# A third FFN pair computed by quarters, and a gate held until after m5's copy, in a one-core encoder block

## The chip, the cores and the metric

The kernel runs on one core of a Trainium2 chip. The metric is the time of one execution on the device, in microseconds. The core's engines are TensorE (PE in the profile, its weight loads PEld), VectorE (DVE), ScalarE (ACT), GpSimd (POOL) and SyncE (SP, which here only issues loads). Each engine runs its own instructions in order and waits on semaphores for the others.

## The reference

One layer over 512 tokens of width 1024, in float32. Two of its stages are gated FFNs with a hidden width of 2816, and the change lies in these:

```python
def _swiglu(x, w_in, w_out):
    gate, up = jnp.split(x @ w_in, 2, axis=-1)
    return (jax.nn.silu(gate) * up) @ w_out
...
h = h + 0.5 * _swiglu(_rmsnorm(h, ffn1_norm[i]), ffn1_w_in[i], ffn1_w_out[i])
...
h = h + 0.5 * _swiglu(_rmsnorm(h, ffn2_norm[i]), ffn2_w_in[i], ffn2_w_out[i])
```

Between them stand a convolution module and gated linear attention, behind them a gated input embedding and a last norm.

## The kernel before

**Split products.** Float32 operands are split in a high and a low part (`high`, `low`, lines 183 and 193): ScalarE casts a weight tile of 128x1024 to its high part, tile wh; VectorE subtracts to get the low part, tile wl. Each product is three matmuls: high by high, high by low, low by high. There are six tiles each of wh and wl, and six raw tiles (wr) into which SyncE loads weights; a raw tile is given back when the last operation that reads it has ended. `added` (line 198) makes the low part without VectorE: ScalarE writes the negated copy of the raw tile into wl, and a transfer issued by GpSimd adds the raw tile to it.

**FFN pairs.** The hidden width is worked through in 11 pairs of 2 x 128 columns. `Left` holds a pair's four weight quarters a11, a12 (gate columns) and a21, a22 (up columns), each for one half of the 1024 inputs. A pair is computed in one of two ways:

- Plain: eight units h0 to h7, each 12 matmuls over all 512 tokens. h0 to h3 make the gate columns, h4 to h7 the up columns; h4 and h6 use a21, h5 and h7 use a22. The gates follow h1 and h3, the product with them h5 and h7, and after h7 `act_parts` splits the pair's result (two ScalarE casts actH, two VectorE subtractions actL).
- By quarters: seven products m1, m2, m6, m7, m5, m4, m3 of 24 matmuls over 256 tokens each, on sums of weights and sums of tokens (`mul`, line 308). `s12` makes s1 = a21 + a22 and s2 = s1 - a11 (tiles sm), `s3_` makes a11 - a21, `s4_` makes a12 - s2, all on VectorE; each sum is then split like a weight. The token sums belong to `Right`: `pieces` are ScalarE copies (tile xg), `sums1` and `sums2` VectorE subtractions, and `split` makes the operands t2, t3, t1 and t4 (a ScalarE cast and a VectorE subtraction for each half).

A bank of PSUM is added into more than once: m1, m6, m5 and m3 go into one bank, and between them ScalarE copies it out (`snap`): as sq after m1, as u2 after m6, as sq again after m5. m7 and m4 go into a second bank; between them VectorE reads it for u (`plus`, line 629). m2 goes into a third; its gate (VectorE g twice, ScalarE's silu s) needs m1's copy.

**Order.** The order on TensorE, VectorE and ScalarE is that of the code, fixed by `Ordered` (line 36). `drive` (line 584) walks a list of units; before a unit it issues the preparations of later units, each a set number of units ahead (`AHEAD` = 4 for a weight's cast and subtraction, 5 for m5's, 6 for the sums, 7 and 9 for loads). Then come the first leftover of the unit before (a gate, say), the unit's own products, its hook, and the other leftovers. Hooks, keyed by unit and pair, carry the token sums.

**The first FFN** (lines 870 to 883) computes pair 0 from the start on as its inputs arrive, pairs 1 and 2 plain and pairs 3 to 10 by quarters; the token sums hang on units of pairs 1 and 2. The product with `w_out` is made in out-pieces (`second`, line 752), four for each group of pairs in `CUTS`, 24 matmuls of 512 tokens each; the four of pairs 0 and 1 stand among pair 2's units. In **the second FFN** (lines 1429 to 1528) pair 0 is plain and pairs 1 to 10 go by quarters; only there is the first pair's gate held back (list `held`), until after m6's copy. Its tokens and weights are prepared beside `plain_block`s just ahead of it.

Of the kernel before, what the change touches and what calls it, by code (L numbers as in the profile page):

```python
# [62 lines left out]
def block_kernel(ctx: ExitStack, tc: tile.TileContext, a: dict, out: bass.AP):  # L63
# [16 lines left out]
    def nm(s):  # L80
        uid[0] += 1
        return f"{s}_{uid[0]}"
# [10 lines left out]
    def tmp(s, w=SEQ, dt=F32, bufs=2):  # L93
        return tp.tile([P, w], dt, tag=s, bufs=bufs, name=nm(s))

    def bank():
        return pp.tile([P, SEQ], F32, tag="mm", bufs=7, name=nm("ps"))

    def aux():
        return pp.tile([P, SEQ], F32, tag="aux", bufs=1, name=nm("ax"))  # L100
# [82 lines left out]
    def high(r3):  # L183

        nk, nc_ = r3.shape[1], r3.shape[2]
        hi = wp.tile([P, 1024], F32R, tag="wh", bufs=6, name=nm("wh"))
        lo = wp.tile([P, 1024], F32R, tag="wl", bufs=6, name=nm("wl"))
        h3 = hi[:, :nk * nc_].rearrange("p (k c) -> p k c", k=nk)
        l3 = lo[:, :nk * nc_].rearrange("p (k c) -> p k c", k=nk)
        act.copy(h3, r3)  # L190
        return h3, l3, r3

    def low(w, engine=dve):
        h3, l3, r3 = w
        engine.tensor_tensor(out=l3, in0=r3, in1=h3.bitcast(F32), op=ALU.subtract)
        return h3, l3

    def added(w):

        h3, l3, r3 = w  # L200
        act.mul(l3, r3, -1.0)
        pool.dma_start(out=l3.bitcast(F32), in_=r3, accum_op=ALU.add)
        return w
# [10 lines left out]
    def ahead(src, c0, ncol):  # L214


        return [[added(w) for w in high4(load(src, 0, DC, c, P))] for c in range(c0, c0 + ncol, P)]
# [41 lines left out]
    def spread(col, copy=True):  # L259

        ps = aux()
        for j in range(TB):
            pe.transpose(ps[:, j * P:(j + 1) * P], col[:, j:j + 1].to_broadcast([P, P]), ident)
        if not copy:
            return ps
        bc = tmp("bc", bufs=1)
        act.copy(bc, ps)
        return bc
# [39 lines left out]
    def mul(ps, w, x, first, last, ks=range(4)):  # L308

        (wh, wl), k0 = w, ks[0]  # L310
        for k in ks:
            xh, xl = x[k]
            for i in range(2):
                cs = slice(i * P, (i + 1) * P)
                o = ps[:, i * HALF:(i + 1) * HALF]
                end = last and k == ks[-1] and i == 1
                pe.matmul(o, wh[:, k - k0, cs], xh, start=(first and k == ks[0] and i == 0), stop=False, skip_group_check=True)
                pe.matmul(o, wh[:, k - k0, cs], xl, start=False, stop=False, skip_group_check=True)
                pe.matmul(o, wl[:, k - k0, cs], xh, start=False, stop=end, skip_group_check=True)

    def two(t):
        return t.rearrange("p (k c) -> p k c", k=2)
# [65 lines left out]
    class Left:  # L388
# [17 lines left out]
        def part(self, name, engine=None):  # L406
# [2 lines left out]
                self.done[name] = low(high(getattr(self, name)), engine or dve)  # L409
            return self.done[name]  # L410

        def add_part(self, *names):

            for name in names:
                self.done[name] = added(high(getattr(self, name)))[:2]
# [21 lines left out]
    ffn1_in = a["ffn1_w_in"][0]  # L437
    hT = [big.tile([P, SEQ], F32, tag="H", bufs=DC, name=nm("h")) for _ in range(DC)]
    hg, xps, xt, squares = [], [], {}, []
# [74 lines left out]
    w1 = Left(ffn1_in, 2)  # L514
# [9 lines left out]
    ps0 = [bank() for _ in range(4)]  # L524
    split_w(0, 1, dve.tensor_copy)
    split_x(0)
    mid = []
# [22 lines left out]
    xb = Right(hg, "ffn1_norm")  # L550
    steps = xb.steps()
# [30 lines left out]
    AHEAD = 4  # L582
# [18 lines left out]
        for f in left:  # L601
            f()

    def ffn(w_in, w_out, x, gname, given, first, rsb, hooks, plain):


        norm = Norm()
# [3 lines left out]
        start = 1 + len(plain)  # L611
        held = []
        end = npair - 1
        pairs = {i: given.get(i) or Left(w_in, 2 * i) for i in range(npair)}

        def row(i):
            return got['rsb'][:, i * HALF:(i + 1) * HALF].unsqueeze(1).to_broadcast([P, 2, HALF])
# [6 lines left out]
        def silu(g):  # L624
            s = tmp("s")
            act.activation(s, g, AF.Silu)
            return s

        def plus(ps, t, i, name):
            o = tmp(name)  # L630
            dve.tensor_tensor(out=o, in0=ps, in1=t, op=ALU.add)
            dve.tensor_tensor(out=two(o), in0=two(o), in1=row(i), op=ALU.mult)
            return o
# [11 lines left out]
        def snap(ps, name, **kw):  # L645
            o = tmp(name, **kw)
            act.copy(o, ps)
            return o
# [16 lines left out]
        def m2(p):  # L665
            p.y = bank()
            mul(p.y, p.part("a12"), x.op["b21"], True, True)

            def gate0():
                p.s0 = silu(plus(p.y, p.a, 0, "g1"))  # L670

            if p is pairs[start] and not plain:
                held.append(gate0)
                return []
            return [gate0]

        def m6(p):
            mul(p.x, p.part("s2"), x.op["t2"], False, False)
            p.u2 = snap(p.x, "u2", bufs=1)
            for f in held:  # L680
                f()
            held.clear()

        def m7(p):
            p.w = bank()
# [2 lines left out]
        def m5(p):  # L688
            mul(p.x, p.part("s1"), x.op["t1"], False, False)
            p.u = plus(p.w, snap(p.x, "sq", bufs=3), 1, "u1")  # L690

        def m4(p):
            mul(p.w, p.part("a22"), x.op["t4"], False, True)
            gated(p, p.s0, plus(p.w, p.u2, 0, "u1"), 0)
# [32 lines left out]
        def unit(kind, i):  # L727
            p = pairs[i]

            def go(run):  # L730
                left = run(p)
                hooks.get((kind, i), lambda *_: None)()
                return left

            if kind[0] == "h":
                j = int(kind[1])
                part, run = (f"a{1 + j // 4}{1 + j % 2}", plain_unit(j)) if j % 4 < 2 else (None, plain_unit(j))
                if part:
                    return [(AHEAD, lambda: p.part(part)), (9, lambda: p.fetch(part))], lambda: go(run)
            else:  # L740
                part, run = USES[kind]
            before = [(AHEAD + (kind == 'm5'), lambda: p.part(part))] if part else []
            if kind in ("m1", "m2"):
                before.append((7, lambda: p.fetch(part)))
            elif kind == "m6":
                before += [(9, lambda: p.fetch("a21", "a22")), (6, p.s12)]
            elif kind in ("m7", "m3"):
                before.append((6, p.s3_ if kind == "m7" else p.s4_))

            return before, lambda: go(run)  # L750
# [80 lines left out]
        for i in range(start, npair):  # L831
# [3 lines left out]
            if i == end:  # L835
                half, rest = second(cut_of[i])
# [30 lines left out]
    w_in = a["w_in"][0]  # L867
    w_ahead = []

    def sums_hooks(x, names, at):  # L870

        h = {}
        for name, key in zip(names, at):
            h[key] = lambda *_, name=name: x.split(name)
        return h

    hooks = sums_hooks(xb, ("t2", "t3", "t1", "t4"), (("h5", 1), ("h7", 1), ("h3", 2), ("m1", 3)))
    hooks.update({("h%d" % (i + 1), 1): f for i, f in enumerate(steps[2:])})
    hooks.update({("m5", 3): lambda *_: made[0](), ("m5", 4): lambda *_: constants(),
                  ("m4", 10): lambda *_: w_ahead.append(ahead(w_in, D_CONV, 2 * P)),  # L880
                  ("last", 4): lambda *_: w_ahead.append(ahead(w_in, 0, 2 * P))})
    hg, norm = ffn(ffn1_in, a["ffn1_w_out"][0], xb, "mix_norm", {0: Left(ffn1_in, 0), 1: w1},
                   (ps0[:2], ps0[2:]), lambda: spread(mid[0]), hooks, (1, 2))
    pool.on = False
    cw, gwu, mean, mask, nbias = made

# [61 lines left out]
    mid = []  # L948
# [10 lines left out]
    rs, rsb = mid  # L959
# [16 lines left out]
    for k0 in range(0, DC, 4):  # L976
        for i in range(2):
            for j in range(4):
                pe.matmul(ps[2 * RANK * j:2 * RANK * (j + 1)], gw[:, k0 + j, :], hg[k0 + j][i].bitcast(F32),
                          start=(k0 == i == 0), stop=(k0 + i == 5), skip_group_check=True)  # L980
# [339 lines left out]
    w0, w1 = wf[0], wf[1]  # L1320
# [40 lines left out]
    norm = Norm()  # L1361
# [57 lines left out]
    hg = nhg  # L1419
# [11 lines left out]
    mid = []  # L1431
    xb = Right(hg, "ffn2_norm")
    steps = xb.steps()
    steps[0]()
    w1.fetch("a21", "a22")
    w2 = wf[2]
# [15 lines left out]
    u1_ = plain_block(w0, 1, 1)  # L1452
    xb.split("t1")
    w1.part("s3")
    hooks = sums_hooks(xb, ("t4",), (("m2", 1),))
    hooks.update({("m7", 10): lambda *_: turn_p(0), ("m5", 10): lambda *_: turn_p(1)})

    w_gate = a["ple_w_gate"][0]
    q11, q21, q12, q22, b11, b21, t2, wproj = ([] for _ in range(8))
# [68 lines left out]
    hg, norm = ffn(ffn2_in, a["ffn2_w_out"][0], xb, "ple_norm", wf, ((g0, u0), (g1_, u1_)), mid[1], hooks, ())  # L1528
# [3 lines left out]
    def of_rows(k, h):  # L1532

        return [tuple(t[:, HS[h]] for t in hg[4 * k + c]) for c in range(4)]

    a11, a12, a21, a22 = of_rows(0, 0), of_rows(1, 0), of_rows(0, 1), of_rows(1, 1)
# [138 lines left out]
    def kept(ps, name, **kw):  # L1675
        o = tmp(name, **kw)
        act.copy(o, ps)
        return o
# [20 lines left out]
    t1, t3 = q11, q12  # L1699
    n2_ = [x for jp in range(2) for x in split_rows(n2, jp)]  # L1700
    project(0)
    m1 = [kept(p_, "sq", bufs=3) for p_ in x_]
# [98 lines left out]
```

## Time and profile before

| | us |
|---|---|
| median of 3 runs (lowest, highest) | 947.86 (947.75, 948.25) |
| the profiled execution | 947.54 |
| its span on the core | 945.8 |
| TensorE busy | 933.3 |
| VectorE busy | 756.9 |
| ScalarE busy | 476.0 |
| mean granted TensorE clock | 0.997 of full speed |

In a row of a timeline stand the start, the duration of one or of the group, the engine, the line (L46, the helper that records every operation, for nearly all), the operation, output<-inputs and the shapes; in brackets the idle time of the engine ahead of it and what ended that. In a table by stretches stand, for each engine, the busy time and the count, then the granted clock, the share of the DMA engines and GB/s. A group's idle time is that of its own engine.

### The profile page before, as it was taken

How to read it: one execution, taken by the hardware profiler on the slowest of the kernel's cores; microseconds unless marked ns; L12 is line 12 of the kernel's file. 1: busy time of each engine (PE TensorE's matmuls, PEld its weight loads, DVE VectorE, ACT ScalarE, POOL GpSimd, SP SyncE). 2: the span in 40 equal slices, each digit the busy share in tenths (PEclk: the TensorE clock that was granted, in tenths of full speed). 3: DMA queues.
4: the chain of work that ended last, by engine and by line, in shares of the span. 5: the costliest groups of instructions: out<-in, count | busy, mean ns of one | idle time of the engine just before them, and what ended most of it. 6: DMA issues, size and time to landing. Idle time of an engine off the chain costs nothing.

```text
span 945.8 us, 14552 instructions
## 1 busy us (share of the span) xinstructions
PE 933.3 (99%) x5842; PEld 830.1 (88%) x5842; DVE 756.9 (80%) x1031; ACT 476.0 (50%) x719; POOL 56.2 (6%) x71
## 2 busy tenths in 40 slices
PE   9999999999999999999999999999999999999996
PEld 7888999999999988788877889999999999998885
DVE  6776887887788566999986788887878787866896
ACT  5752544334443474463564875444434433445882
POOL 0000200000000110001030010000000000000121
PEclk9999999999999999999999999999999999999998
DMA  7532323342223593346552562332243224347463
GB/s 229 181 121 75 95 76 121 95 134 83 97 89 112 145 256 83 77 112 157 134 131 75 151 156 67 118 124 71 89 135 112 67 91 133 97 150 220 91 112 112
DMA packets 107687, 112.90 MB, mean 119 GB/s; under 512 B 5139, under 2 KB 96453, under 8 KB 107620
## 3 DMA queue, kind: packets, MB, share of 16 engines
q1 hardware_dynamic: 101732, 94.67, 32.1%
q0 software_dynamic: 5872, 17.30, 10.2%
q8 instruction: 46, 0.75, 0.3%
q14 instruction: 21, 0.17, 0.1%
q10 hardware_dynamic: 16, 0.00, 0.0%
HBM read 93.61 MB, written 2.10 MB: 101 GB/s over the span
## 4 chain that ended last, share of the span: by engine, by line
PE 96%; DVE 2%; ACT 0%; issue 0%; DMA 0%; POOLq 0%; SPq 0%; DVEq 0%; ACTq 0%
PE ps L46 95%; PE ax L46 1%; DVE wl L46 1%; DMA wr<-in_ffn_w_in 0%; DVE g L46 0%; DVE sm L46 0%; ACT wh L46 0%; ACT s L46 0%; DVE y L46 0%; DVE actL L46 0%; DVE t1L L46 0%; DVE hgL L46 0%; DVE u L46 0%; POOLq L1797 0%; ACT ycH L46 0%
## 5 line engine op out<-in xcount | busy, mean ns | idle before, releaser
L46 PE MATMUL ps<-hgH,wh 128*128 128x256 f32 (+1 forms) x768 | 235.1, 311 | 2.1 <-DVE u L46 1.5
L46 PE MATMUL ps<-hgL,wh 128*128 128x256 f32 (+1 forms) x768 | 234.2, 310 | 0.0
L46 PE MATMUL ps<-hgH,wl 128*128 128x256 f32 (+1 forms) x768 | 233.9, 310 | 0.0
L46 DVE TENSOR_TENSOR wl<-wr,wh 128x1024 fp32r<-128x1024 f32 (+2 forms) x163 | 190.8, 1182 | 48.5 <-ACT wh L46 48.4
L46 ACT CAST wh<-wr 128x1024 fp32r<-128x1024 f32 (+2 forms) x177 | 177.8, 1019 | 34.7 <-PE ps L46 15.1
L46 PEld LDWEIGHTS ps<-hgH,wh 128*128 128x128 f32 x768 | 146.4, 191 | 11.9 <-DVE u L46 1.7
L46 PEld LDWEIGHTS ps<-hgL,wh 128*128 128x128 f32 x768 | 146.3, 191 | 8.0 <-issue 0.2
L46 PEld LDWEIGHTS ps<-hgH,wl 128*128 128x128 f32 x768 | 146.5, 191 | 7.6
L46 PE MATMUL ps<-actH,wh 128*128 128x512 f32 x352 | 137.4, 390 | 0.0
L46 PE MATMUL ps<-actL,wh 128*128 128x512 f32 x352 | 137.3, 390 | 0.0
L46 PE MATMUL ps<-actH,wl 128*128 128x512 f32 x352 | 136.9, 389 | 0.0
L46 ACT ACTIVATE s<-g 128x512 f32<-128x512 f32 x48 | 30.4, 633 | 197.1 <-DVE g L46 197.1
L46 DVE SCALAR_TENSOR_TENSOR cv<-glu,cw,cv 128x502 f32<-128x502 f32 (+24 forms) x120 | 81.1, 734 | 0.6
L46 PEld LDWEIGHTS ps<-actH,wl 128*128 128x128 f32 x352 | 66.1, 188 | 14.0
L46 PEld LDWEIGHTS ps<-actH,wh 128*128 128x128 f32 x352 | 66.2, 188 | 12.9
L46 PEld LDWEIGHTS ps<-actL,wh 128*128 128x128 f32 x352 | 66.2, 188 | 12.5
L46 DVE SCALAR_TENSOR_TENSOR h<-ps,h 128x512 f32<-128x512 f32 x80 | 54.0, 687 | 21.9 <-PE ps L46 21.8
L46 ACT COPY sq<-ps 128x512 f32<-128x512 f32 x40 | 23.3, 585 | 69.7 <-PE ps L46 69.7
L46 DVE TENSOR_TENSOR wl<-sm,wh 128x1024 fp32r<-128x1024 f32 x40 | 48.7, 1222 | 3.0 <-ACT wh L46 2.8
L46 ACT CAST actH<-m 128x512 fp32r<-128x512 f32 x44 | 25.4, 618 | 38.5 <-DVE m L46 38.4
L46 ACT CAST wh<-sm 128x1024 fp32r<-128x1024 f32 x40 | 41.7, 1043 | 5.9 <-DVE sm L46 2.9
L46 PE MATMUL ps<-t1H,wh 128*128 128x256 f32 x144 | 40.8, 284 | 0.0
(267 smaller groups left out, 1741.6 us busy)
## 6 DMA issues: line engine op xcount, KB each, us to landing
wr<-in_ffn_w_in SPq DMA_DIRECT2D x84, 512.0 KB
wr<-in_ffn_w_out SPq DMA_DIRECT2D x32, 512.0 KB
wr<-in_w_in SPq DMA_DIRECT2D x20, 512.0 KB
wl<-wr POOLq DMA_DIRECT2D x15, 512.0 KB, 5.2
wr<-in_ffn_w_out SPq DMA_DIRECT2D x16, 384.0 KB
wr<-in_w_out SPq DMA_DIRECT2D x8, 512.0 KB
wq<-in_ple_w_gate SPq DMA_DIRECT2D x8, 512.0 KB
wl<-wq POOLq DMA_DIRECT2D x8, 512.0 KB, 5.1
```

Source lines behind the costliest of these rows:

```text
L46: inst = call(*args, **kwargs)
```

## The change

In the first FFN `plain` becomes (1,): pair 2 goes by quarters, and the out-pieces of pairs 0 and 1 move behind it, two to a pair. The token sums are set earlier, on units h0, h2, h3 and h4 of pair 1, with pair 2's weight sums `s12` and `s3_` in the same hooks; t4 moves to m1 of pair 2. Three low parts go over to `add_part`: a21 of pair 1 (h4), a12 and a22 of pair 2 (m2, m4; six units ahead). a22 of pair 1 is cast three units ahead of h5 (`cast`), and its subtraction (`rest`) stands in h2's hook. In both FFNs the gate of the first pair by quarters is now held, and is issued behind m5's copy and u instead of behind m6's copy. In the second FFN a12 of pair 2 is made by `add_part`, ahead of pair 0's gates; VectorE's subtraction for it, after m2 of pair 1, falls away.

```diff
@@ class Left
+        def cast(self, name):
+            self.half = high(getattr(self, name))
+
+        def rest(self, name):
+            self.done[name] = low(self.half)
@@ ffn
-    def ffn(w_in, w_out, x, gname, given, first, rsb, hooks, plain):
+    def ffn(w_in, w_out, x, gname, given, first, rsb, hooks, plain, adds=()):
...
-            if p is pairs[start] and not plain:
+            if p is pairs[start]:
                 held.append(gate0)
                 return []
             return [gate0]
 
         def m6(p):
             mul(p.x, p.part("s2"), x.op["t2"], False, False)
             p.u2 = snap(p.x, "u2", bufs=1)
-            for f in held:
-                f()
-            held.clear()
 
         def m7(p):
             p.w = bank()
             mul(p.w, p.part("s3"), x.op["t3"], True, False)
 
         def m5(p):
             mul(p.x, p.part("s1"), x.op["t1"], False, False)
             p.u = plus(p.w, snap(p.x, "sq", bufs=3), 1, "u1")
+            for f in held:
+                f()
+            held.clear()
...
                 if part:
-                    return [(AHEAD, lambda: p.part(part)), (9, lambda: p.fetch(part))], lambda: go(run)
+                    make = p.add_part if (kind, i) in adds else p.part
+                    first_ = [(3, lambda: p.cast(part))] if (kind, i) in hooks.get("cast", ()) else [(AHEAD, lambda: make(part))]
+                    return first_ + [(9, lambda: p.fetch(part))], lambda: go(run)
             else:
                 part, run = USES[kind]
-            before = [(AHEAD + (kind == 'm5'), lambda: p.part(part))] if part else []
+            if (kind, i) in adds:
+                before = [(AHEAD + 2, lambda: p.add_part(part))]
+            else:
+                before = [(AHEAD + (kind == 'm5'), lambda: p.part(part))] if part else []
@@ first FFN
-    hooks = sums_hooks(xb, ("t2", "t3", "t1", "t4"), (("h5", 1), ("h7", 1), ("h3", 2), ("m1", 3)))
-    hooks.update({("h%d" % (i + 1), 1): f for i, f in enumerate(steps[2:])})
+    hooks = sums_hooks(xb, ("t2", "t3", "t1", "t4"), (("h2", 1), ("h3", 1), ("h4", 1), ("m1", 2)))
+    w2 = Left(ffn1_in, 4)
+    hooks.update({"cast": {("h5", 1)},
+                  ("h0", 1): lambda *_: [f() for f in steps[2:4]],
+                  ("h2", 1): lambda *_: [w1.rest("a22"), steps[4](), xb.split("t2")],
+                  ("h3", 1): lambda *_: [xb.split("t3"), w2.s12()],
+                  ("h4", 1): lambda *_: [xb.split("t1"), w2.s3_()]})
...
-    hg, norm = ffn(ffn1_in, a["ffn1_w_out"][0], xb, "mix_norm", {0: Left(ffn1_in, 0), 1: w1},
-                   (ps0[:2], ps0[2:]), lambda: spread(mid[0]), hooks, (1, 2))
+    hg, norm = ffn(ffn1_in, a["ffn1_w_out"][0], xb, "mix_norm", {0: Left(ffn1_in, 0), 1: w1, 2: w2},
+                   (ps0[:2], ps0[2:]), lambda: spread(mid[0]), hooks, (1,), {("h4", 1), ("m2", 2), ("m4", 2)})
@@ ahead of the second FFN
     xb.split("t1")
     w1.part("s3")
+    w2.add_part("a12")
```

## The prediction

> **What bounds the kernel now.** I read the page's busy times first, then TensorE's own waits, then the timeline of each engine through the two openings that the change edits.
>
> ```profile
> PE 933.3 (99%) x5842; PEld 830.1 (88%) x5842; DVE 756.9 (80%) x1031; ACT 476.0 (50%) x719; POOL 56.2 (6%) x71
> PE ps L46 <- DVE u L46: 1.5, 1, 1.5
> 75.40:97.20 21.80, 21.80 (x98) 18.05 (x97) 14.52 (x16) 5.34 (x7) 0.00 (x0) 1.00 0.15 48
> 97.20:120.00 22.80, 22.80 (x189) 22.58 (x188) 21.00 (x26) 10.84 (x16) 4.94 (x6) 1.00 0.31 94
> ```
>
> TensorE sets the time (99%); inside both FFNs its only wait is one of 1.5 us on VectorE, in the second. But VectorE is no free cover: in the table by stretches (after PE and PEld comes DVE) it is busy 14.5 of 21.8 us in a stretch of plain products and out-pieces, and 21.0 of 22.8 us where quarter products begin. So TensorE gains whatever products it loses, unless VectorE or ScalarE, in their fixed order, come too late.
>
> **The removed products.** TensorE's timeline, column one the start:
>
> ```profile
> 87.94 0.39 PE L46 MATMUL ps<-hgL,wh 128*128 128x512 f32 x1
> 97.00 0.39 PE L46 MATMUL ps<-actH,wl 128*128 128x512 f32 x1
> 97.23 0.28 PE L46 MATMUL ps<-hgH,wh 128*128 128x256 f32 x1
> 105.74 0.28 PE L46 MATMUL ps<-hgH,wl 128*128 128x256 f32 x1
> ```
>
> 40 wide matmuls lie between the first two starts: 0.2267 us each. 71 narrow ones between the last two: 0.120 us. A plain pair is 96 wide, 21.76 us; a pair by quarters is 7 products of 24 narrow, 2.88 us each, 20.16 us. **Gain 1.60 us**, not the eighth (2.7 us) that the count of products promises. [...]
>
> **The first opening: who is late.** Pair 2's weight sums and the token sums must now be ready within pair 1's eight plain units instead of pairs 1 and 2. Pair 1's units start every 2.72 us from 34.56, so unit h5 is due at 45.4, m1 of pair 2 at 53.6. The prices, from ScalarE's and VectorE's timelines:
>
> ```profile
> 33.13 1.05 ACT L46 CAST wh<-wr 128x1024 fp32r<-128x1024 f32 x1
> 34.84 0.59 ACT L46 COPY bc<-ax 128x512 f32<-128x512 f32 x1 [0.66 <-PE ax L46]
> 40.65 1.05 ACT L46 CAST wh<-wr 128x1024 fp32r<-128x1024 f32 x1
> 41.60 1.70 ACT L46 ACTIVATE xg<-h,vcol 128x256 f32<-128x256 f32 x4
> 53.73 1.13 ACT L46 CAST t2H<-xg 128x512 fp32r<-128x512 f32 x2
> 545.24 1.06 ACT L46 ACTIVATE wl<-wr 128x1024 fp32r<-128x1024 f32 x1
> 546.20 1.03 ACT L46 CAST wh<-wr 128x1024 fp32r<-128x1024 f32 x1
> 40.01 1.46 DVE L46 TENSOR_TENSOR actL<-m,actH 128x512 fp32r<-128x512 f32 x2
> 42.87 2.14 DVE L46 TENSOR_TENSOR xg<-xg,xg 128x512 f32<-128x512 f32 x3
> 44.93 0.68 DVE L46 TENSOR_TENSOR g<-ps,bc 128x512 f32<-128x512 f32 x1
> 45.53 0.68 DVE L46 TENSOR_TENSOR xg<-xg,xg 128x512 f32<-128x512 f32 x1
> 62.91 2.36 DVE L46 TENSOR_TENSOR wl<-wr,wh 128x1024 fp32r<-128x1024 f32 x2 [0.26 <-ACT wh L46]
> 87.16 1.22 DVE L46 TENSOR_TENSOR sm<-wr,wr 128x1024 f32<-128x1024 f32 x1
> 88.41 1.23 DVE L46 TENSOR_TENSOR sm<-sm,wr 128x1024 f32<-128x1024 f32 x1
> ```
>
> From one start to the next: weight cast 0.95, negated copy 0.96, four token pieces 1.6, half-size cast 0.53 on ScalarE; half-size operation 0.6, chain of three token sums 2.06, weight subtraction 1.14, sum pair 2.4 on VectorE.
>
> Step 1, h5's low part. The negated copy of a21 (the add_part of h4) pushes the copy bc from 34.84 to 35.0, and with it the first gates by 0.2. Pair 0's act casts end ScalarE's string at 40.85; then come all eight pieces (3.2, to 44.05) and only then the cast of a22, done at 45.1. VectorE has by then finished actL (41.6), three sums (43.6), one more (44.2) and a gate (44.9), so its subtraction runs 45.1 to 46.35. TensorE wants it at h5's third matmul, 45.9. **0.4 us late.** It was ready at 42.96 before (cast at 40.65 plus both).
>
> Step 2, m1's low part. From 46.3: three sums (48.3), t2's two low parts (49.5). t3's casts stand on ScalarE behind t2's second cast (waiting for a sum done at 47.6, ends 48.2) and the cast and negated copy of a12: 50.1. So t3's low parts end 51.9, s1 and s2 54.3, and a11 of pair 2 at 55.5. TensorE, already 0.4 late, wants it at 54.3. **1.2 to 1.3 us late.**
>
> Step 3, the snapshot that m5 needs. m5 adds into the bank that m6 left, so ScalarE must have copied it first (u2). VectorE goes on: gate (56.0), then t1's low parts behind ScalarE's silu and two casts (57.3 to 58.5), s3 (59.7), a11 of pair 3 (60.8), u and m of h5 (62.1), three weight subtractions (65.5), u and m of h7: 66.95. ScalarE waits there for its second act cast, in front of u2. After it in order: the cast (0.53), cast and negated copy of a22 (0.95, 0.96), cast of a12 (0.95), snapshot of m1 (0.48), cast of an out-piece (0.95), u2 itself (0.59): 72.4. TensorE finishes m1 (restarted at 55.3), m2, m1, m6, m7, 14.4 us, at 69.7. **2.7 us late.**
>
> Step 4. The raw tile of the out-piece is given back only when its subtraction ends (about 74), and the load of pair 3's a22 takes its place; with 3 to 4 us of load VectorE's s1 of pair 3 starts at 77 to 78 instead of at 74, and the lag runs through to u2 of pair 3, ahead of m5 of pair 3. By the same addition that is 1.0 us late; it is a long chain, so I hold 0 to 2 open. From then on the out-pieces (5.4 us of TensorE with little for VectorE) let both engines catch up.
>
> These four come to 5.4 us; each is set by VectorE's or ScalarE's clock, so a mistake in an earlier one is paid back by the next. The transfers that replace subtractions are POOL's:
>
> ```profile
> wl<-wr POOLq DMA_DIRECT2D x15, 512.0 KB, 5.2
> ```
>
> a21's is issued near 35.4 and landed at 41 to 42, due 43.2; a12's is issued at 50.5, landed at 56 to 57, due 58.4 with the stalls above. Were one 2 us slower, step 3's time, which does not hang on it, would absorb it. Bounds for them: 0 and 1 us.
>
> **The second opening.**
>
> ```profile
> 559.04 0.28 PE L46 MATMUL ps<-hgH,wh 128*128 128x256 f32 x1
> 579.07 0.28 PE L46 MATMUL ps<-hgH,wl 128*128 128x256 f32 x1
> 580.85 0.39 PE L46 MATMUL ps<-hgH,wh 128*128 128x256 f32 x1 [1.50 <-DVE u L46]
> 562.77 0.63 ACT L46 ACTIVATE s<-g 128x512 f32<-128x512 f32 x1 [1.89 <-DVE g L46]
> 576.23 0.63 ACT L46 ACTIVATE s<-g 128x512 f32<-128x512 f32 x1 [4.89 <-DVE g L46]
> 578.66 0.57 ACT L46 COPY sq<-ps 128x512 f32<-128x512 f32 x1
> 579.13 1.04 ACT L46 CAST wh<-sm 128x1024 fp32r<-128x1024 f32 x1
> 590.47 0.58 ACT L46 COPY u<-ps 128x512 f32<-128x512 f32 x1
> 571.19 1.22 DVE L46 TENSOR_TENSOR wl<-wr,wh 128x1024 fp32r<-128x1024 f32 x1
> 574.73 0.68 DVE L46 TENSOR_TENSOR g<-ps,sq 128x512 f32<-128x512 f32 x1
> 580.11 0.69 DVE L46 TENSOR_TENSOR u<-ps,sq 128x512 f32<-128x512 f32 x1
> 580.83 0.69 DVE L46 TENSOR_TENSOR u<-u,bc 128x512 f32<-128x512 f32 x1
> ```
>
> m4 adds into the bank that u at 580.11 reads; it starts at 580.85 instead of 579.19: the 1.66 us to be won. The change takes the subtraction at 571.19 (1.14) and the gate at 574.73 (1.32) out of u's way. Against that, the new cast of a12 needs a seventh wh tile of six: a21's and a22's are given back, but a11, a12 of pair 1, a11 of pair 2, a22, s2 and s3 are held, so it waits for m1 to end (559.04 + 2.88 + 0.16 = 562.1) and with its negated copy starts the silu of 562.77 at 564.0. Hence VectorE is 1.1 us later at first, m1's snapshot ends at 568.1 where m6 is due at 567.7 (0.4 late), and u still comes at 578.2 to 578.9, in time for m4 at 579.6. But the held silu now stands behind u, at 581.0, in front of two weight casts (the first was at 579.13). Their subtractions, the next gates and so ScalarE's u2 of pair 2 move from 590.47 to 591.6, ending 592.2. TensorE's m5 of pair 2 waits for that: it started at 580.85 + 4 x 2.88 = 592.4 and now starts at 592.2. **Gain 0.2 us**; bounds 0.5 lost and 1.66 won.
>
> **Sum.** The profiled execution took 947.54 us (span 945.8). 947.54 - 1.60 + 5.4 - 0.2 = 951.1; the median of the runs lies 0.32 above that execution, so **951.4 us**, 0.4% slower. What a run can tell from no change here is about 0.2%, that is 945.96 to 949.76.
>
> **Rivals.** (a) Everything is covered: no new wait and the old one gone, 947.86 - 1.60 - 1.66 = 944.6. For it: VectorE is idle a third of the stretch from 75.4. Against: the new work does not lie there but between 41 and 72, where I find it contiguous; it would need VectorE or ScalarE about 4 us earlier at step 3. (b) Only steps 1 and 2 bite, ScalarE's snapshots not, because its casts leave ahead of the act cast: 947.86 - 1.60 + 1.7 - 0.2 = 947.8, no change. For it: in every steady pair the snapshots follow their product at once; against: the order is by hand and the snapshot is behind five operations. (c) The long stall at step 3 costs TensorE its clock:
>
> ```profile
> 579.00:581.00 2.00, 0.50 (x4) 0.29 (x4) 1.97 (x4) 2.00 (x3) 0.00 (x0) 1.00 0.83 264
> 940.00:945.80 5.80, 0.00 (x0) 0.00 (x0) 1.90 (x6) 0.00 (x0) 0.47 (x1) 0.52 0.36 137
> ```
>
> The granted clock (third from the right) stayed 1.00 over the 1.5 us wait, and is 0.52 in the 5.8 us after the last matmul. A stall of 2.7 us lies between. If the clock halves for as long as the stall lasted, narrow products at half rate lose 1.4 us, for twice as long 2.7: 952.8 to 954.1. [...]
>
> **How the numbers follow.** Forecast 0.67 (its own range 949.8 to 952.8, from step 4's bounds and 0.5 us on the rest); (a) 0.08; (b) 0.15; (c) 0.10. Faster 0.08, no change 0.15, slower 0.77. The range leaves out (a) and the tails: 947.6 to 953.9.
>
> **What would show it.** In the changed trace, TensorE waits for VectorE's wl near 46 and 55, and for ScalarE's snapshot (the row of u<-ps ends when TensorE restarts) near 72; the wait at 580.85 is gone, and a shorter one stands before m5 of the next pair. Wrong it is if the first opening has no wait over 0.5 us, if the first act cast of h7 comes before 66, or if narrow products run faster than 0.120 us.

## The result, and the profile after

| | before | after |
|---|---|---|
| median (us) | 947.84 | 954.08 |
| its runs | 947.86, 948.25, 947.75, 947.82 | 954.99, 953.24, 954.91, 952.60 |
| profiled execution (span) | 947.54 (945.8) | 954.99 (953.3) |
| ratio of after to before, 95% interval | | 1.0062 [1.005, 1.0075] |

The change makes the kernel 0.6% slower. The page's busy times, and the table of TensorE's waits (total, times, longest) of the changed kernel:

```profile
PE 936.8 (98%) x5914; PEld 835.5 (88%) x5914; DVE 761.9 (80%) x1037; ACT 483.8 (51%) x729; POOL 57.7 (6%) x75
PE ps L46 <- ACT u L46: 4.0, 3, 2.4
PE ps L46 <- DVE wl L46: 1.3, 2, 1.1
```

Before, the only wait inside the FFNs was 1.5 us on VectorE's u. That row is gone; in its place stand three waits on ScalarE's snapshot u and two on low parts. Where they stand, in TensorE's timeline of the changed kernel:

```profile
47.97 0.39 PE L46 MATMUL ps<-hgL,wh 128*128 128x512 f32 x1
48.57 0.50 PE L46 MATMUL ps<-hgH,wl 128*128 128x512 f32 x1 [0.21 <-DVE wl L46]
...
57.88 0.39 PE L46 MATMUL ps<-hgH,wl 128*128 128x256 f32 x1 [1.08 <-DVE wl L46]
...
72.02 0.28 PE L46 MATMUL ps<-t3H,wl 128*128 128x256 f32 x1
74.72 0.38 PE L46 MATMUL ps<-t1H,wh 128*128 128x256 f32 x1 [2.43 <-ACT u L46]
74.95 0.28 PE L46 MATMUL ps<-t1L,wh 128*128 128x256 f32 x1
...
104.39 0.28 PE L46 MATMUL ps<-t3H,wl 128*128 128x256 f32 x1
105.32 0.38 PE L46 MATMUL ps<-t1H,wh 128*128 128x256 f32 x1 [0.65 <-ACT u L46]
...
575.57 0.39 PE L46 MATMUL ps<-t2H,wh 128*128 128x256 f32 x1 [0.20 <-ACT sq L46]
...
599.80 0.39 PE L46 MATMUL ps<-t1H,wh 128*128 128x256 f32 x1 [0.94 <-ACT u L46]
```

These are, in order, h5, m1, m5 of pair 2, m5 of pair 3, and in the second FFN m6 of pair 1 and m5 of pair 2. A wait costs more than its bracket says: from 72.02 to 74.72 are 2.70 us where 0.12 belong, so 2.58, and the next start is 0.11 late too. Counted so, the four of the first opening cost 0.48, 1.24, 2.69 and 0.91 us.

Two things in this execution are no waits. The first is the clock behind the long wait. In the table by stretches, granted clock third from the right:

```profile
74.00:75.00 1.00, 0.28 (x2) 0.28 (x3) 1.00 (x2) 0.67 (x2) 0.00 (x0) 1.00 1.04 201
75.00:76.00 1.00, 1.00 (x8) 1.00 (x8) 1.00 (x2) 0.76 (x1) 0.00 (x0) 0.72 1.06 201
76.00:77.00 1.00, 1.00 (x7) 1.00 (x6) 0.29 (x1) 0.29 (x1) 0.00 (x0) 0.50 0.02 0
...
78.00:79.00 1.00, 1.00 (x7) 1.00 (x7) 0.00 (x0) 0.00 (x0) 0.00 (x0) 0.57 0.86 219
79.00:80.00 1.00, 1.00 (x10) 1.00 (x10) 0.00 (x0) 0.59 (x1) 0.00 (x0) 1.00 0.82 232
```

A mean of 0.72 means half speed for 0.56 of that microsecond, so the clock fell at 75.44; by the 0.57 it rose at 78.86, 3.42 us later. Narrow products started 0.214 us apart there (75.60 to 78.59, 14 of them) instead of 0.120: 1.47 us lost.

The second is the start, which the change does not touch: TensorE's instructions there are the same in both kernels. TensorE before, then after:

```profile
5.10 0.60 PE L46 MATMUL ax<-ident 128*128 128x128 f32 x4
6.30 1.17 PE L46 MATMUL ps<-hgH,wh 128*128 128x512 f32 x4 [0.60 <-DVE wh L46]
...
34.20 0.60 PE L46 MATMUL ax<-ident,rs 128*128 128x128 f32 x4
```

```profile
5.17 1.06 PE L46 MATMUL ax<-ident 128*128 128x128 f32 x4
6.73 2.04 PE L46 MATMUL ps<-hgH,wh 128*128 128x512 f32 x4 [0.49 <-DVE wh L46]
8.57 1.91 PE L46 MATMUL ps<-hgH,wl 128*128 128x512 f32 x4
...
36.39 0.60 PE L46 MATMUL ax<-ident,rs 128*128 128x128 f32 x4
```

Four wide products take 2.04 us instead of 1.17: TensorE ran at half speed (by the trace's record of clock changes until 10.60 us, before until 5.00), and by the transposes at 36.39 it was 2.19 us behind. Below I call this the late start; it comes in all kernels, by 0 to 2.2 us. Each profile gives its own size, so I compare **profiled executions less their late start**: before 947.54, after 952.80. Of the 5.3 us between them the first opening holds 5.4: there the same product starts 2.19 us later than before at the opening's start and 7.58 at its end. The second FFN gives 0.1 back.

### The profile page after: what moved, and what is told of

Its sections match the earlier page's. It is cut to its first block, busy times and chain, and to the rows that moved or that the text cites. A ratio compares the mean times of both kernels' runs of the same rounds, so it can differ in the third digit from the quotient of the medians.

```text
span 953.3 us, 14722 instructions
## 1 busy us (share of the span) xinstructions
PE 936.8 (98%) x5914; PEld 835.5 (88%) x5914; DVE 761.9 (80%) x1037; ACT 483.8 (51%) x729; POOL 57.7 (6%) x75
## 4 chain that ended last, share of the span: by engine, by line
PE 87%; DVE 5%; ACT 3%; issue 2%; DMA 1%; POOLq 0%; SPq 0%; ACTq 0%; DVEq 0%
PE ps L46 86%; DVE wl L46 2%; ACT wh L46 1%; PE ax L46 1%; DVE g L46 1%; DMA wr<-in_ffn_w_in 1%; ACT xg L46 1%; DVE u L46 1%; DVE sm L46 1%; DMA wl<-wr 0%; ACT s L46 0%; ACT wl L46 0%; DVE m L46 0%; DVE wr L46 0%; DVE xg L46 0%
## 5 line engine op out<-in xcount | busy, mean ns | idle before, releaser
L46 PE MATMUL ps<-hgH,wh 128*128 128x256 f32 (+1 forms) x768 | 232.4, 308 | 0.5 <-DVE wh L46 0.5
L46 PE MATMUL ps<-hgH,wl 128*128 128x256 f32 (+1 forms) x768 | 231.5, 307 | 1.3 <-DVE wl L46 1.3
L46 PE MATMUL ps<-hgL,wh 128*128 128x256 f32 (+1 forms) x768 | 230.8, 306 | 0.0
L46 DVE TENSOR_TENSOR wl<-wr,wh 128x1024 fp32r<-128x1024 f32 (+2 forms) x160 | 187.4, 1182 | 45.1 <-ACT wh L46 45.0
L46 DVE TENSOR_TENSOR wl<-sm,wh 128x1024 fp32r<-128x1024 f32 x42 | 51.0, 1221 | 5.8 <-ACT wh L46 5.6
L46 PE MATMUL ps<-t1H,wh 128*128 128x256 f32 x152 | 44.1, 290 | 4.0 <-ACT u L46 4.0
L46 ACT CAST wh<-sm 128x1024 fp32r<-128x1024 f32 x42 | 43.7, 1042 | 5.0 <-DVE sm L46 2.1
L46 PE MATMUL ps<-t1H,wl 128*128 128x256 f32 x152 | 43.8, 288 | 0.0
```

The source lines that it names most:

```text
L46: inst = call(*args, **kwargs)
```

## The experiments

Each kernel is the changed one with the edit shown, unless it says otherwise; medians stand beside the median of before in the same session (947.77 to 947.95).

**e1 and e2, the two FFNs apart.** e1 takes the second FFN's edits out, e2 puts only them into the kernel before:

```diff
 # e2, against the kernel before
 def m6(p):
     p.u2 = snap(p.x, "u2", bufs=1)
-    for f in held:
-        f()
-    held.clear()
...
 def m5(p):
     p.u = plus(p.w, snap(p.x, "sq", bufs=3), 1, "u1")
+    for f in held:
+        f()
+    held.clear()
...
     w1.part("s3")
+    w2.add_part("a12")
```

> The changed kernel with its second FFN as before (gate held until after m6's copy, no add_part of a12). Theory: the two parts add up, and the second FFN is worth 0.26 us of gain by the two traces (0.31 more ahead of m6, 1.57 less ahead of m4, 1.0 more ahead of m5 of pair 2). So 954.08 + 0.26 = 954.3, all of it from the first opening: waits of about 0.2, 1.1, 2.4 and 0.65 us, half clock for 3.4 us behind the third, and the 1.5 us wait ahead of m4 back in the second FFN. Rival: the second FFN's edits gain their whole 1.6 and something else behind them costs 1.3: then about 955.7 here. An execution whose first products run at half speed up to about 10.7 us is 2.2 us longer in either case.

> The kernel before with only the second FFN's edits (gate held until after m5's copy, add_part of a12). Theory: VectorE's and ScalarE's orders hand the wait on, so 947.84 - 0.26 = 947.6, with about 0.2 us of wait ahead of m6, none ahead of m4, about 0.9 ahead of m5 of pair 2. Rival: the wait ahead of m4 goes and nothing takes its place, 946.2. The first FFN is as in the kernel before: no wait, clock 1.00 throughout.

Measured: e1 952.86 (profile 953.55, late start 0.77, so 952.78); e2 947.72 against 947.77, ratio 1.0001 [0.9992, 1.001] (profile 948.04 less 0.48: 947.56). The loss is the first opening's alone, and the second FFN's edits change nothing that a run can tell. e1 and the changed kernel agree although their late starts differ (0.77 and 2.19), which speaks for taking them off. e1's 954.3 was too high since it stood on a median with late starts in it. In e2 the 1.5 us wait is gone, and TensorE's timeline has two others for it:

```profile
568.53 0.38 PE L46 MATMUL ps<-t2H,wh 128*128 128x256 f32 x1 [0.20 <-ACT sq L46]
...
592.75 0.39 PE L46 MATMUL ps<-t1H,wh 128*128 128x256 f32 x1 [0.94 <-ACT u L46]
```

**e3, the product first.** VectorE's u and m of h7 ahead of two weight subtractions (unit 8 is m1 of pair 2):

```diff
-    def drive(units):
+    def drive(units, early=()):
...
-        for jobs, (_, run) in zip(todo, units):
+        for n, (jobs, (_, run)) in enumerate(zip(todo, units)):
+            if n in early:
+                for f in left[:1]:
+                    f()
...
-            for f in left[:1]:
-                f()
+            if n not in early:
+                for f in left[:1]:
+                    f()
...
-        drive(units)
+        drive(units, (8,) if plain else ())
```

> The changed kernel with VectorE's u and m of h7 issued ahead of the two weight subtractions (for m5 and m7 of pair 2) that stood in front of them. Theory: the wait ahead of m5 of pair 2 is VectorE's order, carried to ScalarE's u2 by the act cast. u and m come about 2.3 us earlier, the wait falls from 2.4 to about 0.2 us, TensorE keeps its clock there (1.5 us saved), and as TensorE is earlier, u2 of pair 3 is later against it: its wait grows from 0.65 to about 1.9. Sum -2.3 - 1.5 + 1.2 = -2.6: 954.08 becomes 951.5 (953.0 if that wait costs the clock in its turn). Rival 1: u2 is held by ScalarE's own casts, and the order of VectorE changes nothing, 954.1. Rival 2: the half clock belongs to the narrow products, not to the wait, and stays: 953.0 with the clock low near 75 although the wait there is gone.

**e4, a cast behind u2.**

```diff
-                return [(7, get), (AHEAD, make)], run
+                return [(7, get), (AHEAD - (f0 == n == 0 and bool(plain)), make)], run
```

> The changed kernel with ScalarE's cast of the first out-piece moved from in front of u2 of pair 2 to behind it. Theory: the wait ahead of m5 of pair 2 falls by that cast's 0.95 us, from 2.4 to 1.5, and the wait ahead of m5 of pair 3 grows by the same, from 0.65 to 1.6, since VectorE's chain ahead of that one doesn't move. The idle time as a sum is unchanged; what changes is its longest piece. If the clock falls only for a wait that fills most of one of the clock's 3.4 us steps, it stays at 1.00 and the time falls by the 1.5 us that half speed cost: 952.6. Rival: the clock follows the idle time as a sum, or any wait over 1 us: 954.1, with one or two stretches of half clock.

Measured: e3 953.19 (profile less late start 953.09), e4 955.24 (955.33). Less the late start neither is faster than the changed kernel's 952.80. TensorE's timeline of e3, and the stretches behind its second row:

```profile
70.51 0.39 PE L46 MATMUL ps<-t1H,wh 128*128 128x256 f32 x1 [0.16 <-ACT u L46]
...
102.27 0.39 PE L46 MATMUL ps<-t1H,wh 128*128 128x256 f32 x1 [2.93 <-ACT u L46]
```

```profile
103.00:104.00 1.00, 1.00 (x11) 1.00 (x10) 1.00 (x2) 1.00 (x2) 0.00 (x0) 0.92 0.00 0
104.00:105.00 1.00, 1.00 (x6) 1.00 (x6) 1.00 (x2) 0.12 (x1) 0.00 (x0) 0.50 0.00 0
...
107.00:108.00 1.00, 1.00 (x8) 1.00 (x9) 0.77 (x2) 1.00 (x2) 0.00 (x0) 0.87 0.98 318
```

The same two views of e4:

```profile
71.81 0.38 PE L46 MATMUL ps<-t1H,wh 128*128 128x256 f32 x1 [1.49 <-ACT u L46]
...
103.31 0.58 PE L46 MATMUL ps<-t1H,wh 128*128 128x256 f32 x1 [2.94 <-ACT u L46]
```

```profile
102.00:103.00 1.00, 0.00 (x0) 0.00 (x0) 1.00 (x3) 1.00 (x2) 0.00 (x0) 0.74 0.00 0
103.00:104.00 1.00, 0.69 (x3) 0.69 (x4) 1.00 (x2) 1.00 (x2) 0.00 (x0) 0.50 0.00 0
...
109.00:110.00 1.00, 1.00 (x8) 1.00 (x8) 0.55 (x1) 1.00 (x2) 0.00 (x0) 0.85 0.98 315
```

The order of VectorE did carry the wait at pair 2 (2.43 to 0.16), and a 1.49 us wait kept the clock. e3 came out near the 953.0 that it gave for a second wait that costs the clock. But all that TensorE won there it lost again at pair 3, whose wait grew to 2.9 us, not to the 1.6 to 1.9 expected. Less the late start, m5 of pair 3 restarts at 103.13 in the changed kernel, 103.04 in e1 and 103.09 in e4: one point, whether TensorE lost 2.7 us ahead of m5 of pair 2 and ran at half speed for 3.4 us behind it (changed kernel, e1) or lost 1.8 and kept its clock (e4). So u2 of pair 3 is the end of a chain of VectorE, ScalarE and a load that does not ask when TensorE comes. The half clock at 75 had hidden 1.5 us of that wait and cost nothing itself. In e3 half speed lay behind the restart (3.42 us), in e4 all but its first 0.83 us did (6.82 in all), and there it cost 1.4 and 2.6 us.

**e5 and e6, the chain made shorter.** e5 adds unit 18, the one behind m3 of pair 2, to e3's edit: `drive(units, (8, 18) ...)`. e6:

```diff
-                    first_ = [(3, lambda: p.cast(part))] if (kind, i) in hooks.get("cast", ()) else [(AHEAD, lambda: make(part))]
+                    first_ = [(4, lambda: p.cast(part))] if (kind, i) in hooks.get("cast", ()) else [(AHEAD, lambda: make(part))]
...
-                before = [(AHEAD + 2, lambda: p.add_part(part))]
+                before = [(AHEAD + 1 + (kind == 'm4'), lambda: p.add_part(part))]
...
-                  ("h0", 1): lambda *_: [f() for f in steps[2:4]],
-                  ("h2", 1): lambda *_: [w1.rest("a22"), steps[4](), xb.split("t2")],
+                  ("h0", 1): steps[2],
+                  ("h1", 1): lambda *_: [steps[3](), w1.rest("a22")],
+                  ("h2", 1): lambda *_: [steps[4](), xb.split("t2")],
```

> The changed kernel with VectorE's product of h7 ahead of two weight subtractions, as in e3, and the product behind m3 of pair 2 ahead of the next weight subtraction as well. Theory: TensorE's restart at m5 of pair 3 is set by VectorE's chain (load of a22, weight sums, product, act casts, u2) whatever TensorE lost before; the two products shorten that chain by 1.1 and 2.0 us, and leave waits of 1.2 us and less, so the clock stays at 1.00. From 952.8 (the changed kernel without the half-speed start) 3.1 off: 949.7. Rival: the half clock and the wait ahead of m5 of pair 2 are losses of their own beside the chain; then both go and 2.4 + 1.5 + 0.65 come off: 948.2.

> The changed kernel with the two short waits mended: a22 of pair 1 cast after the first four token pieces and subtracted in h1's hook (0.48 us ahead of h5), and add_part of a12 of pair 2 one unit later, behind the casts of t3 (1.24 us ahead of m1 of pair 2). Theory: VectorE's string itself moves forward by 1.6 us, since it had waited 1.2 us for those casts, so everything behind it does too, and the long wait and the half clock stay as they are: 952.8 - 1.6 = 951.2. Rival: the later waits are set by something else than this string (ScalarE, loads) and grow by what is saved: 952.8.

Measured: e5 950.21, e6 951.42. TensorE's timeline of e5, then of e6, at m5 of pair 2 and of pair 3:

```profile
70.43 0.39 PE L46 MATMUL ps<-t1H,wh 128*128 128x256 f32 x1 [0.16 <-ACT u L46]
...
99.83 0.39 PE L46 MATMUL ps<-t1H,wh 128*128 128x256 f32 x1 [0.94 <-ACT u L46]
```

```profile
70.92 0.39 PE L46 MATMUL ps<-t1H,wh 128*128 128x256 f32 x1 [2.42 <-ACT u L46]
...
101.15 0.38 PE L46 MATMUL ps<-t1H,wh 128*128 128x256 f32 x1 [0.29 <-ACT u L46]
```

| less late start | restart of m5, pair 3 | time | difference of the two |
|---|---|---|---|
| changed kernel | 103.13 | 952.80 | 849.67 |
| e1 | 103.04 | 952.78 | 849.74 |
| e5 | 99.65 | 949.30 | 849.65 |
| e6 | 101.13 | 950.74 | 849.61 |
| e3 (half clock behind the restart) | 102.01 | 953.09 | 851.08 |
| e4 (twice as long) | 103.09 | 955.33 | 852.24 |

Over a range of 3.5 us the time follows that restart within about 0.1 us, and only half clock behind it adds to it. e6 keeps the 2.4 us wait and the half clock behind it, as its table by stretches shows, and is 2.1 us faster all the same:

```profile
72.00:73.00 1.00, 1.00 (x6) 1.00 (x6) 0.48 (x1) 0.48 (x1) 0.00 (x0) 0.50 0.36 66
```

Both rivals fall: e5 stays 1.1 us above its rival's 948.2 even less the late start, and e6 gains 2.1 us where its rival had none and its theory 1.6.

**e7 to e9, the second FFN mended, and everything together.** In e7 ScalarE casts a12 of pair 3 behind u2 of pair 2:

```diff
-            before = [(AHEAD + (kind == 'm5'), lambda: p.part(part))] if part else []
+            before = [(AHEAD + (kind == 'm5') - (kind == 'm2' and i == 3 and not plain), lambda: p.part(part))] if part else []
```

e8 is e5, e6 and e7 with the first out-piece's cast and subtraction one unit earlier (`AHEAD + (f0 == n == 0 and bool(plain))`); e9 is e2 with e7's edit, so pair 2 of the first FFN stays plain.

> The changed kernel with ScalarE's cast of a12 of pair 3 of the second FFN behind u2 of pair 2 instead of in front of it. Theory: the wait of 0.94 us (1.1 with the restart) ahead of m5 of pair 2 is that cast's time and goes, and nothing follows: 952.8 - 0.95 = 951.85. Rival: it moves on to the next product that waits, as the wait ahead of m4 did: 952.8.

> The changed kernel with the edits of e5, e6 and e7, and the cast and subtraction of the first out-piece one unit earlier, so that its raw tile is free sooner for the load of a22 of pair 3. Theory: no wait over 0.5 us is left in the first opening, no half clock; the first FFN's 5.4 us of waits fall to 0.6, of the 1.6 us of fewer products 1.0 is kept, and the second FFN gains 1.2: 945.7 without a half-speed start, 2.1 faster than the kernel before. Rival: VectorE and ScalarE together are the bound of the opening and hand the waits on to pairs 3 and 4: about 948.

> The kernel before (pair 2 plain) with the second FFN's edits of the change and the cast of a12 of pair 3 behind u2 of pair 2: e8 without anything in the first FFN. Theory: the second FFN is worth 0.26 + 0.95 = 1.2 us, so 947.85 - 1.2 = 946.65, and the difference to e8 (946.09) is what the third pair by quarters is worth once nothing waits for it: 0.6, up to the 1.6 us of its fewer products. Rival: the mended second FFN alone makes e8's gain, 946.1 here.

Measured: e7 952.05, e8 946.09 with ratio 0.9979 [0.997, 0.9988], e9 946.54 with ratio 0.9984 [0.9975, 0.9993]. All three lie within 0.4 us of their theory (951.85, 945.7, 946.65). e8 is 0.2% faster than the kernel before; what its earlier out-piece alone is worth was not run. TensorE's waits of e8, and where the last of them stands:

```profile
PE ps L46 <- DVE wh L46: 0.6, 1, 0.6
...
PE ps L46 <- ACT sq L46: 0.2, 1, 0.2
PE ps L46 <- ACT u L46: 0.2, 1, 0.2
```

```profile
70.20 0.28 PE L46 MATMUL ps<-t3H,wl 128*128 128x256 f32 x1
70.64 0.38 PE L46 MATMUL ps<-t1H,wh 128*128 128x256 f32 x1 [0.17 <-ACT u L46]
```

The first of these waits (DVE wh) is the start's, ahead of the first product. Less the late starts e9 stands at 946.44 and e8 at 945.59: with little left to wait for, the third pair by quarters is worth 0.9 us. The lowest runs of the two (946.32 and 945.42) lie as far apart; the intervals of their ratios overlap.

**e10, the start.** e8 with `warm_up(7)` for `warm_up(4)` ahead of the first product.

> e8 with three more transposes of the identity in the gap ahead of the first product (7 instead of 4); they compute nothing that is used. [...] With the gap filled, full speed comes at about 7 to 8 us at the latest: the slowest runs fall from 947.6 to about 946.5, the fastest stay at 945.5, the median about 945.8. Rival: the late rise has to do with the loads (the casts that TensorE waits for), and the spread of 2 us stays, or the transposes delay the first product and all runs are 0.3 us longer.

Measured: 945.77 (945.43 to 946.62), ratio 0.9976 [0.9967, 0.9985]; e8 had 945.42 to 947.57. The fastest stayed, the slowest fell by 0.95. TensorE in e10:

```profile
5.18 0.98 PE L46 MATMUL ax<-ident 128*128 128x128 f32 x7
6.16 1.20 PE L46 MATMUL ps<-hgH,wh 128*128 128x512 f32 x4
7.20 1.08 PE L46 MATMUL ps<-hgH,wl 128*128 128x512 f32 x4
```

The gap ahead of the first product is gone, and it runs at full speed: the first four take 1.20 us. That a filled gap brings full speed by 7 to 8 us was an estimate, and the trace does not decide it: the clock of this execution rose at 5.27 us, before the filled gap begins; e9, with 4 transposes, starts as early (late start 0.12). Nor do the runs: the medians (946.09 and 945.77) are 0.3 us apart with overlapping intervals, and the narrower spread hangs on one run of e8 (947.57), without which its runs end at 946.37. Whether the transposes help stays open.

## Why the prediction was right, and where its size was off

The direction and the mechanism held: TensorE lost more to VectorE's and ScalarE's fixed order than the fewer products gave. The size was at the edge: the median of 954.08 lies 0.2 us above the stated range (947.6 to 953.9), while the ratio of 1.0062 lies just inside it (953.9 / 947.86 is 1.0064), and 952.80, the execution less its late start, lies well inside. Step by step:

- **The removed products**, 1.60 us: e8 against e9 shows 0.85 with 0.68 us lost in e8's first opening at the third product of m1 and at m5 of pair 2 (from 70.20 to 70.64 are 0.44 us where 0.12 belong), so 1.5 in all. The trace's 0.120 us was the right price.
- **Steps 1 to 3** (0.4, 1.2 to 1.3, 2.7 us): 0.48, 1.24, 2.69. e6 took the first two away and e3 all but 0.32 of the third, each by the operation that the working named. ScalarE's timeline after, for the third:

```profile
65.53 0.62 ACT L46 CAST actH<-m 128x512 fp32r<-128x512 f32 x1
69.30 0.62 ACT L46 CAST actH<-m 128x512 fp32r<-128x512 f32 x1 [3.15 <-DVE m L46]
74.09 0.58 ACT L46 COPY u<-ps 128x512 f32<-128x512 f32 x1
```

Less the late start the second act cast waits until 67.11 (the working had 66.95) and u2 ends at 72.48 (72.4). One sign of being wrong was badly named, though: the first of the two act casts started at 63.34, before 66, because it reads the product of h5; the one that the working counts on is the second.

- **Step 4 is the term that was mis-sized.** It reads "with 3 to 4 us of load VectorE's s1 of pair 3 starts at 77 to 78 instead of at 74", and from there 1.0 us, 0 to 2 held open. VectorE's timeline after:

```profile
75.07 1.22 DVE L46 TENSOR_TENSOR wl<-wr,wh 128x1024 fp32r<-128x1024 f32 x1
80.89 1.23 DVE L46 TENSOR_TENSOR sm<-wr,wr 128x1024 f32<-128x1024 f32 x1 [4.60 <-DMA wr<-in_ffn_w_in]
```

The raw tile came free at 76.29, less the late start 74.10, as foretold (about 74). The sum began 4.6 us later, not 3 to 4: 78.70. TensorE's wait behind it reads 0.91 only because the half clock had made TensorE 1.47 us late; the chain was 2.4 us late, where 1.0 was in the sum and 2 the upper bound. That is most of the 1.7 us between 951.1 and 952.80. The load's part in it is read from this one trace: no run changed the load alone.

- **Rival (c)** named the half clock and its price (1.4 us; 1.47 measured), and its 952.8 met the number, yet for another reason than it gave: in this kernel the half clock took the place of a wait and added nothing, as e4 and e6 show. That the number fits is luck: step 4's shortfall is about as large as the price of the half clock. Its chance of 0.10 was the author's estimate: the longest wait of before behind the first product, 1.5 us, had kept the clock (1.00 from 579 to 581). Here 2.4 us of idle time (72.30 to 74.72) cost it.
- **The second opening**, 0.2 us of gain: the same products compared before and after start 0.46 us later from m6 of pair 1 on, 1.76 earlier from m4 on and 1.20 later from m5 of pair 2 on. In sum 0.1 is won, too little for e2's runs to tell. The 0.26 that e1, e2 and e9 reckoned with came from the brackets, which leave out the restarts. The new wait goes with the cast that stands in front of u2: with e7's edit the loss of 1.20 falls to 0.26.
- **Rivals (a) and (b)** fell with the first trace.
- **The start** was not thought of. It is in the median of 954.08 with about 1.3 us and in the profiled execution with 2.19.

## What to carry to other kernels

When a wait goes and the time does not, look for the next product that waits on the same engines, and compare its absolute restart, less whatever moved the whole trace. If that stays, as it did here (103.13, 103.04 and 103.09 us in the changed kernel, e1 and e4), a chain that does not ask for the waiting engine sets the time, and shortening that chain pays (e5 and e6: the restart 3.5 and 2.0 us earlier, the time 3.5 and 2.1 less). A wait on a copy can be cured in the order of the engine that feeds it (here two products moved ahead of weight subtractions, e5: the wait ahead of m5 of pair 2 went from 2.43 to 0.16 us, and m5 of pair 3 restarted 3.5 us earlier), without faster work. And a loss that stood ahead of such a restart was free here (half clock of 3.42 us in the changed kernel), while the same loss behind it counted in full (e3: 1.4 us).

## What was unexpected in the hardware

**The clock moves in steps.** Half speed lasted 3.42 us in the changed kernel (75.44 to 78.86; 3.413 in the trace's record of clock changes) and in e3 (103.84 to 107.26), and 6.82 in e4 (102.48 to 109.30). By that record, from the first rise to the last fall lie 935.25 us in the kernel before, 274 times this 3.413, and from the first rise to the fall behind the long wait 64.85 in the changed kernel, 19 times. The clock fell behind steps that were idle only in part: the 3.41 us ahead of each fall held 2.42 us of idle time in the changed kernel, about 2.1 in e4, 1.95 in e1 and 1.84 in e3 (from the end of its last product, 99.34, the step from 100.43 was idle until 102.27), while no 1.5 us wait (before, e4) took the clock. And a step that was busy for three quarters did not bring it back (e4, 102.48 to 105.89, idle until 103.31), while the clock came back behind one that was idle for its first 0.47 us (e1, 72.84 to 76.25). Where between these the limits lie no run shows.

**The start differs between executions.** Executions of one kernel spread over 2 us (before: 947.17 to 949.78 over all sessions), and the late start follows the moment at which the clock rises first. In seven of the twelve traces it rose at 4.9 to 6.4 us (late start -0.1 to 0.48, the most with the longest gap ahead of the first product, 1.01 us in e2), in e4 and e1 at 6.91 and 7.99 (0.22 and 0.77), and in e7, e8 and the changed kernel at 9.9 to 10.6 (1.74 to 2.19). TensorE's instructions there are the same in all but e10. Counted back from the rise in steps of 3.41 us, the last step but one of the three late ones ended at 6.5 to 7.2 and took in some of the gap ahead of the first product (0.49 us in the changed kernel, 6.23 to 6.73); the clock did not rise at its end. That the place of the steps against this gap makes a start late is a reading of these traces that no run shows.
